# A quarter of the weight groups: the low part from a negated copy and two accumulating DMAs

## The chip, the cores and the metric

The kernel runs on one core of a Trainium2 chip. A core has five engines that run their own instruction queues side by side: TensorE (PE in the profile, its weight loads PEld), VectorE (DVE), ScalarE (ACT), GpSimd (POOL) and SyncE (SP, which here only issues DMAs). Sixteen DMA engines move data between HBM and the on-chip memory SBUF. Products accumulate in PSUM. DMAs can be issued from the queues of SP, ACT and POOL; an instruction at the head of a queue that waits holds up all that stands behind it.

The metric is the time of one execution in device microseconds (us). Two runs of the kernel before gave 1782.39 and 1782.95 us, median 1782.67.

## What is computed

One decoder layer for 256 tokens of width 2048, all in float32: a SwiGLU feed-forward network (FFN) of hidden width 5632, a mixer (pooling and gated linear attention behind one joint projection), and a second FFN. Cut to its frame:

```python
def swiglu(h, w_in, w_out):
    gu = h @ w_in                                   # 2048 x 11264
    gate, up = gu[..., :D_FF], gu[..., D_FF:]
    return (jax.nn.silu(gate) * up) @ w_out         # 5632 x 2048

h = h + 0.5 * swiglu(rmsnorm(h, ffn1_norm[l]), ffn1_w_in[l], ffn1_w_out[l])
u = rmsnorm(h, mix_norm[l]) @ w_in_mix[l]           # 2048 x 4112
...
h = h + jnp.concatenate([y_pool, y_gla], axis=-1) @ w_out_mix[l]
h = h + 0.5 * swiglu(rmsnorm(h, ffn2_norm[l]), ffn2_w_in[l], ffn2_w_out[l])
return rmsnorm(h, final_norm)
```

Nearly all of the work is products of 256 tokens with large weight matrices, and each weight is read from HBM once.

## The kernel before

**Split products.** TensorE takes float32 operands as two `float32r` parts: `hi` is the value rounded to 12 significant bits, `lo` the rest, so that `hi + lo` is the value. Each product is accumulated in PSUM as `a_hi*hi + a_hi*lo + a_lo*hi`, where `a` stands for the activations and `hi`, `lo` for the weights. The activations are the stationary operand (128 features by 128 tokens), the weights stream past them, 512 columns at a time.

**Groups.** A weight group is two adjacent K tiles (`KG = 2`, 256 rows) of 512 columns, 512 KB. `weights()` (from line 69) fetches one: line 73 issues one DMA from SP's queue into `raw`, line 86 makes `hi` with a rounding copy on ScalarE (a CAST in the profile), line 87 makes `lo = raw - hi` with a subtraction on VectorE. `raw`, `hi` and `lo` (`wr_`, `wh_`, `wl_` in the profile) come from a pool with `bufs=4`: each has four buffers in turn, and the fifth group's copy has to wait until the first group's buffer is free. `hi` and `lo` come free when TensorE has finished the group, `raw` when the copy and the subtraction have read it.

**Products.** `project()` (line 98) goes over the groups of one 512-column chunk. For each it calls `weights()` and then issues, for both token tiles and both K tiles, the three matmuls of line 110: 12 matmuls a group, in the order hi, lo, hi for the first K tile, then the second, for the first token tile, then the same for the second token tile. A product over K = 2048 has 8 groups, one over K = 5632 has 22.

**Stages.** First FFN: for each of 11 column chunks a `gate` and an `up` product (`f1g`, `f1u`), then four chunks of the way out (`ps_h`, 22 groups each; `residual()`, line 250). Mixer: products `mgr` (336 columns), `mk`, `mq`, `mv`, `mg` (352 columns), `mp` of 8 groups each, the last three twice, with small work between them, then its way out (four chunks of 8 groups, again `ps_h`). Second FFN: `f2g`, `f2u` and `ps_h` as in the first. The very first product has its first group cut in two. In all that makes 633 groups. In the last chunk of the last product the final six groups are held in buffers of another pool (`hold`), so that the token tiles can be finished one after the other.

**GpSimd** has little to do: a power in each row factor (line 154), small input DMAs (lines 310 to 321 and 512 to 514), the key product `ktail` (line 385), the final gains' DMAs and scaling (lines 573 and 580), and six multiplications with them (line 268).

The order of the instructions on each engine is set by the tile framework's scheduler from the program order and its own estimate of the times; semaphores guard every tile that is shared between engines or with a DMA.

Of the kernel before, what the change touches and what calls it, by code (L numbers as in the profile page):

```python
"""Macaron decoder layer (SwiGLU, pooling + gated-linear-attention mixer, SwiGLU) on one core.

Every large product takes float32 operands as two float32r parts that add up to them exactly
(hi = the value rounded to 12 significant bits, lo = the rest) and accumulates
hi*hi + hi*lo + lo*hi in PSUM. Activations are stationary (features on the partitions, tokens in
the columns), weights stream past them 512 columns at a time. The RMSNorm's per-token factor
commutes with the product and is applied where its result leaves PSUM; the gain is applied where
the activations are transposed.
"""
# [8 lines left out]
F32 = mybir.dt.float32  # L18
# [4 lines left out]
ALU = mybir.AluOpType  # L23
PSUM = bass.MemoryType.PSUM

P = 128
T = 256
# [23 lines left out]
def layer(ctx: ExitStack, tc: tile.TileContext, io):  # L51
# [13 lines left out]

# [1 line left out]
    last_load = [None]  # L67

    def weights(w, rows, c0, cw, name, hold):
        """The K tiles `rows` (adjacent) of w's columns c0..c0+cw as (hi, lo)."""  # L70
        n = len(rows)
        raw = wpool.tile([P, KG, CW], F32, tag="wraw", name=f"wr_{name}")
        dma = nc.sync.dma_start(
            out=raw[:, :n, :cw],
            in_=w[rows[0] * P : (rows[0] + n) * P, c0 : c0 + cw].rearrange(
                "(k p) c -> p k c", p=P
            ),
        )
        last_load[0] = dma.ins
        if hold:  # L80
            hi = block([P, KG, CW], F32R, f"wh_{name}")
            lo = block([P, KG, CW], F32R, f"wl_{name}")
        else:
            hi = wpool.tile([P, KG, CW], F32R, tag="whi", name=f"wh_{name}")
            lo = wpool.tile([P, KG, CW], F32R, tag="wlo", name=f"wl_{name}")
        nc.scalar.copy(out=hi[:, :n, :cw], in_=raw[:, :n, :cw])  # L86
        nc.vector.tensor_tensor(  # L87
            out=lo[:, :n, :cw],
            in0=raw[:, :n, :cw],
            in1=hi[:, :n, :cw].bitcast(F32),  # L90
            op=ALU.subtract,
        )
        return hi, lo
# [4 lines left out]
    def project(act, groups, w, c0, cw, name, apart=0, midway=None):  # L98
        """act.T @ w[:, c0:c0+cw] for both token tiles, in PSUM; act(kt) gives (hi, lo) [P, T].
        Over the last `apart` groups the first token tile is finished ahead of the second, and  # L100
        the second's left half ahead of its right; midway() is called behind the fourth group."""
        ps = [ps_acc.tile([P, CW], F32, tag="acc", name=f"ps_{name}_{t}") for t in range(NT)]
# [28 lines left out]

# [1 line left out]
    h = [hpool.tile([P, D], F32, tag=f"h{t}", name=f"h{t}") for t in range(NT)]  # L133
# [6 lines left out]
    def scaled_split(hi, lo, src, col):  # L140
        """hi + lo = src * col (per partition); hi, lo float32r, src [P, n]."""
        nc.scalar.activation(out=hi, in_=src, func=AF.Copy, scale=col)  # L142
        nc.vector.scalar_tensor_tensor(
            out=lo, in0=src, scalar=col, in1=hi.bitcast(F32), op0=ALU.mult, op1=ALU.subtract
        )

    def rms_factor(ss, n, cols, name):
        """(ss / n + EPS) ** -0.5 for [P, cols]; one Newton step on top of the power."""
        v = small.tile([P, cols], F32, tag=f"rv{cols}", name=f"{name}_v")
# [19 lines left out]
    def row_factor(ss, name):  # L169
        """ss [P, NT, 4]: sums of squares by token tile and column chunk."""  # L170
        tot = small.tile([P, NT], F32, tag="tot", name=f"{name}_tot")
        nc.vector.tensor_reduce(out=tot, in_=ss, axis=mybir.AxisListType.X, op=ALU.add)
        return rms_factor(tot, D, NT, name)

    # Products of nothing bring TensorE's clock up while the first loads are on their way.
    zeros = tmp.tile([P, CW], BF16, tag="sil", name="zeros")
# [4 lines left out]

# [1 line left out]
    neg_half = const.tile([P, 8], F32, name="neg_half")  # L183
# [12 lines left out]
    def transposed_rows(src, hi, lo, cols, name):  # L196
        """hi, lo [P, 4, T] from src[t] [P, 512] (token-major), times cols [P, 4]."""
        for k2 in range(2):
            tp = ps_t.tile([P, 2, T], F32, tag="tp", name=f"tp_{name}_{k2}")
            for k in range(2):  # L200
                for t in range(NT):
                    kk = k2 * 2 + k
                    nc.tensor.transpose(  # L203
                        tp[:, k, t * P : (t + 1) * P], src[t][:, kk * P : (kk + 1) * P], ident
                    )
            for k in range(2):
                kk = k2 * 2 + k
                scaled_split(hi[:, kk, :], lo[:, kk, :], tp[:, k, :], cols[kk])

    def ffn_in(w, act, row, name, first=None):  # L210
        """The gated hidden activations; row() gives the row factors once the second product is
        under way."""
        g_hi, g_lo = [], []
# [36 lines left out]
    def residual(act, order, w, factor, gain, name, extra=None):  # L250
        """h += factor * act.T @ w; the new h's transposed parts and row factors."""
        hi, lo = new_hT(name) if gain is not None else (None, None)
# [23 lines left out]

    # ================= first FFN =================
    # x arrives transposed, group by group with the first weights, and behind them as it is.
    first = [[0], [1]] + [[k, k + 1] for k in range(2, KD, 2)]
# [33 lines left out]

    # ================= mixer =================
    w_in = io["w_in_mix"]
# [9 lines left out]

    # decay: gate_lr and the tail of the output gate
    gsil = [block([P, HEADS * DV], F32, f"gsil{t}") for t in range(NT)]
# [17 lines left out]
    for t in range(NT):  # L345
# [3 lines left out]
        z.append(zt)  # L349
    # log_sigmoid(z) = min(z, 0) - ln(1 + exp(-|z|))  # L350
    nc.scalar.activation(out=e, in_=e, func=AF.Exp, scale=-1.0)
# [5 lines left out]

    # exp of the cumulated log decays: transposed (E1, and E2 for its inverse), and of what is
    # left of the chunk behind a token (token-major). tri holds 1/16 where it isn't zero.
    E1 = block([P, HEADS, T], F32, "E1")  # L360
# [17 lines left out]

    # keys
    ps = project(hact, kd, w_in, O_K, CW, "mk")  # L380
# [22 lines left out]

    # queries
    ps = project(hact, kd, w_in, O_Q, CW, "mq")
# [8 lines left out]

    # scores, transposed (keys on the partitions), masked to j <= i within a chunk
    sT = block([P, NT, HEADS, P], F32, "sT")
# [9 lines left out]

    # values
    v = [block([P, HEADS * DV], F32, f"v{t}") for t in range(NT)]
# [6 lines left out]

    # states in front of chunks 1..3
    st = [block([P, HEADS, DV], F32, f"st{n}") for n in range(1, 4)]
# [21 lines left out]

    # the rest of the output gate  # L460
    for c in range(2):
# [6 lines left out]

    # attention outputs, normalized and gated
    y_hi, y_lo = [None] * 4, [None] * 4  # L470
    y = [block([P, HEADS * DV], F32, f"y{t}") for t in range(NT)]
    for t in range(NT):
        so = small.tile([P, HEADS], F32, tag="so", name=f"so{t}")
        po = []
        for hp in range(2):
            o = ps_t.tile([P, 2, DV], F32, tag="tp", name=f"o{t}_{hp}")
            for j in range(2):
# [3 lines left out]
                for cc in range(2):  # L481
                    n = 2 * t + cc
                    if n == 0:
                        continue  # nothing precedes chunk 0
                    nc.tensor.matmul(
# [20 lines left out]

    # pooling: the windows' means minus the token are a product with a banded matrix
    band = [block([P, 2, 3 * P], F32, f"band{i}") for i in range(2)]
# [14 lines left out]
    for i in range(2):  # L523
# [8 lines left out]
        for j in range(2):  # L532
            pp = ps_t.tile([P, 2, T], F32, tag="tp", name=f"pp{i}_{j}")
            for c in range(2):
# [3 lines left out]
                )  # L538
                # Windows reach REACH tokens into the second tile: the columns before it are
                # overwritten, those of the reach added to.  # L540
                nc.tensor.matmul(
# [26 lines left out]

    # ================= second FFN and the final norm =================
    g = ffn_in(io["ffn2_w_in"], hact, lambda: rstd, "f2")  # L570
# [6 lines left out]

    # gf holds the gains over -2, as the Newton step gives -2 times the row factor.
    for n in range(4):
        nc.gpsimd.tensor_scalar_mul(gf[n], gf[n], -0.5)  # L580

    def finish(ps, ss):
        """The last column chunk, by halves; the row factors and the result."""
        half = CW // 2
# [52 lines left out]
def _constants(np):  # L637
    """Matrices that depend on shapes alone: cumulation within a chunk (with the decay's 1/16), and
    trailing-window means minus the token, both with the summed token on the partitions."""
    s, t = np.arange(P)[:, None], np.arange(P)[None, :]  # L640
# [53 lines left out]
```

## Time and profile before

| what | value |
|---|---|
| time, median of 2 runs | 1782.67 us |
| span of the profiled execution, first to last instruction | 1780.9 us |
| mean granted TensorE clock | 0.999 of full speed |
| VectorE's subtractions in `weights()` | 633, 768 us in all |
| ScalarE's rounding copies in `weights()` | 633, 659 us in all |
| GpSimd busy | 35.1 us |
| DMA engines busy (mean of 16), rate | 60%, 190 GB/s |
| moved by DMA | 338 MB, of it 3.06 MB from GpSimd's queue |

The profile is one execution recorded on the chip; the time of that execution itself was not given apart from its span, which is 1.8 us under the median of the timed runs. In a row such as "L86 ACT CAST wh_h<-wr_h ... x208 | 218.9, 1054 | 301.4 <-PE ps_h L110 274.5" stand the line of the kernel, the engine and its operation, output and input tile, the count, the busy time in us, the mean of one in ns, and behind the second bar the time the engine was idle before these instructions with what ended most of it. In the table of waits a row is "who waits <- for whom: us in total, times, longest". In the tables of a tile or line, a row gives the count, the least, median and greatest duration in ns and the start of the first and the last in us. "DMA to landing" counts from the issue of a DMA until its data is there. A stretch of time is given as from:to, its length, the busy time of each engine with the number of its instructions, the granted TensorE clock, the share of the DMA engines' time and the rate in GB/s. TensorE's matmuls overlap: one is shown with 389 ns, but a new one starts every 227 ns.

### The profile page before, as it was taken

How to read it: one execution, taken by the hardware profiler on the slowest of the kernel's cores; microseconds unless marked ns; L12 is line 12 of the kernel's file. 1: busy time of each engine (PE TensorE's matmuls, PEld its weight loads, DVE VectorE, ACT ScalarE, POOL GpSimd, SP SyncE). 2: the span in 40 equal slices, each digit the busy share in tenths (PEclk: the TensorE clock that was granted, in tenths of full speed). 3: DMA queues.
4: the chain of work that ended last, by engine and by line, in shares of the span. 5: the costliest groups of instructions: out<-in, count | busy, mean ns of one | idle time of the engine just before them, and what ended most of it. 6: DMA issues, size and time to landing. Idle time of an engine off the chain costs nothing.

```text
span 1780.9 us, 20687 instructions
## 1 busy us (share of the span) xinstructions
PE 1768.4 (99%) x8086; PEld 1467.1 (82%) x8086; DVE 894.8 (50%) x902; ACT 791.2 (44%) x911; POOL 35.1 (2%) x40
## 2 busy tenths in 40 slices
PE   9999999999999999999999999999999999999998
PEld 6888888888888888878978888888888888888886
DVE  5544444444555445544455554444444555554454
ACT  6444444444444444454445544444444444443443
POOL 0000000000000000000010000000000000200000
PEclk9999999999999999999999999999999999999999
DMA  9666666666565655555554566666666666766653
GB/s 310 202 189 189 189 190 189 189 189 189 190 190 190 197 190 189 175 171 171 173 193 145 188 188 189 189 190 189 189 189 189 189 189 190 215 194 193 192 196 133
DMA packets 176449, 338.01 MB, mean 190 GB/s; under 512 B 10807, under 2 KB 19255, under 8 KB 176096
## 3 DMA queue, kind: packets, MB, share of 16 engines
q1 hardware_dynamic: 174976, 333.10, 59.5%
q0 software_dynamic: 944, 3.06, 0.6%
q8 instruction: 63, 1.03, 0.2%
q10 hardware_dynamic: 432, 0.55, 0.1%
q14 instruction: 34, 0.28, 0.0%
HBM read 334.56 MB, written 2.10 MB: 189 GB/s over the span
## 4 chain that ended last, share of the span: by engine, by line
PE 98%; issue 0%; DMA 0%; DVE 0%; ACT 0%; SPq 0%; POOLq 0%; POOL 0%; DVEq 0%
PE ps_h L110 31%; PE ps_f2g L110 13%; PE ps_f2u L110 13%; PE ps_f1u L110 13%; PE ps_f1g L110 13%; PE ps_mp L110 3%; PE ps_mv L110 2%; PE ps_mg L110 2%; PE ps_mk L110 1%; PE ps_mq L110 1%; PE ps_mgr L110 1%; PE f2tp L240 1%; PE f1tp L240 1%; PE tp_h L203 0%; DMA wr_f1g<-in_ffn_w_in 0%
## 5 line engine op out<-in xcount | busy, mean ns | idle before, releaser
L87 DVE TENSOR_TENSOR wl_h<-wr_h,wh_h 128x1024 fp32r<-128x1024 f32 x208 | 256.8, 1236 | 269.9 <-ACT wh_h L86 269.7
L86 ACT CAST wh_h<-wr_h 128x1024 fp32r<-128x1024 f32 x208 | 218.9, 1054 | 301.4 <-PE ps_h L110 274.5
L87 DVE TENSOR_TENSOR wl_f2u<-wr_f2u,wh_f2u 128x1024 fp32r<-128x1024 f32 x88 | 107.8, 1225 | 131.5 <-ACT wh_f2u L86 131.5
L87 DVE TENSOR_TENSOR wl_f1u<-wr_f1u,wh_f1u 128x1024 fp32r<-128x1024 f32 x88 | 107.8, 1225 | 129.2 <-ACT wh_f1u L86 129.1
L87 DVE TENSOR_TENSOR wl_f2g<-wr_f2g,wh_f2g 128x1024 fp32r<-128x1024 f32 x88 | 107.8, 1225 | 102.1 <-ACT wh_f2g L86 102.1
L87 DVE TENSOR_TENSOR wl_f1g<-wr_f1g,wh_f1g 128x1024 fp32r<-128x1024 f32 (+1 forms) x89 | 108.0, 1213 | 98.9 <-ACT wh_f1g L86 98.5
L86 ACT CAST wh_f2g<-wr_f2g 128x1024 fp32r<-128x1024 f32 x88 | 92.8, 1055 | 126.8 <-PE ps_f2u L110 66.6
L86 ACT CAST wh_f2u<-wr_f2u 128x1024 fp32r<-128x1024 f32 x88 | 92.7, 1053 | 122.6 <-PE ps_f2u L110 66.9
L86 ACT CAST wh_f1g<-wr_f1g 128x1024 fp32r<-128x1024 f32 (+1 forms) x89 | 93.0, 1045 | 119.1 <-PE ps_f1u L110 63.2
L86 ACT CAST wh_f1u<-wr_f1u 128x1024 fp32r<-128x1024 f32 x88 | 92.6, 1052 | 116.1 <-PE ps_f1u L110 61.9
L110 PE MATMUL ps_f1g<-wh_f1g,xT_hi 128*128 128x512 f32 x352 | 137.1, 394 | 2.5 <-ACT xT_hi L142 2.4
L110 PE MATMUL ps_h<-wh_h,f2hi 128*128 128x512 f32 (+1 forms) x364 | 139.2, 382 | 0.0
L110 PE MATMUL ps_h<-wh_h,f2lo 128*128 128x512 f32 (+1 forms) x364 | 139.1, 382 | 0.0
L110 PE MATMUL ps_h<-wl_h,f2hi 128*128 128x512 f32 (+1 forms) x364 | 139.1, 382 | 0.0
L110 PE MATMUL ps_f2g<-wh_f2g,h_hi 128*128 128x512 f32 x352 | 138.0, 392 | 0.0
L110 PE MATMUL ps_h<-wh_h,f1hi 128*128 128x512 f32 x352 | 137.3, 390 | 0.0
L110 PE MATMUL ps_h<-wl_h,f1hi 128*128 128x512 f32 x352 | 137.2, 390 | 0.0
L110 PE MATMUL ps_f2g<-wh_f2g,h_lo 128*128 128x512 f32 x352 | 137.1, 389 | 0.0
L110 PE MATMUL ps_f2g<-wl_f2g,h_hi 128*128 128x512 f32 x352 | 137.1, 389 | 0.0
L110 PE MATMUL ps_h<-wh_h,f1lo 128*128 128x512 f32 x352 | 137.0, 389 | 0.0
L110 PE MATMUL ps_f1u<-wl_f1u,xT_hi 128*128 128x512 f32 x352 | 136.9, 389 | 0.0
L110 PE MATMUL ps_f1u<-wh_f1u,xT_lo 128*128 128x512 f32 x352 | 136.9, 389 | 0.0
(225 smaller groups left out, 3323.8 us busy)
## 6 DMA issues: line engine op xcount, KB each, us to landing
wr_h<-in_ffn_w_out SPq DMA_DIRECT2D x176, 512.0 KB, 3.9
wr_f1u<-in_ffn_w_in SPq DMA_DIRECT2D x88, 512.0 KB, 3.5
wr_f2g<-in_ffn_w_in SPq DMA_DIRECT2D x88, 512.0 KB, 3.4
wr_f2u<-in_ffn_w_in SPq DMA_DIRECT2D x88, 512.0 KB, 3.4
wr_f1g<-in_ffn_w_in SPq DMA_DIRECT2D x87, 512.0 KB, 3.5
wr_h<-in_w_out_mix SPq DMA_DIRECT2D x32, 512.0 KB, 4.0
wr_mv<-in_w_in_mix SPq DMA_DIRECT2D x16, 512.0 KB, 3.6
wr_mp<-in_w_in_mix SPq DMA_DIRECT2D x16, 512.0 KB, 4.5
```

Source lines behind the costliest of these rows:

```text
L86: nc.scalar.copy(out=hi[:, :n, :cw], in_=raw[:, :n, :cw])
L87: nc.vector.tensor_tensor(out=lo[:, :n, :cw], in0=raw[:, :n, :cw], in1=hi[:, :n, :cw].bitcast(F32), op=ALU.subtract,)
L110: nc.tensor.matmul(ps[t][:, c], a[:, s], b[:, j, c], start=kt == first and i == 0, stop=kt == last and i == 2, skip_group_check=c.start > 0,)
L240: nc.tensor.transpose(tp[:, k, :], a[:, k * P : (k + 1) * P], ident)
```

## The change

Every fourth call of `weights()` that isn't held no longer subtracts on VectorE. Instead ScalarE writes `-hi` into `lo` behind the rounding copy, and two DMAs from GpSimd's queue, one for each K tile, read the weights from HBM a second time and add them to `lo` (`accum_op=ALU.add`), which leaves `w - hi` there. The other three quarters of the groups are treated as before. The diff, without the comments and docstrings that it also drops:

```diff
     last_load = [None]
+    count = [0]
 
     def weights(w, rows, c0, cw, name, hold):
         n = len(rows)
         raw = wpool.tile([P, KG, CW], F32, tag="wraw", name=f"wr_{name}")
...
         nc.scalar.copy(out=hi[:, :n, :cw], in_=raw[:, :n, :cw])
+        count[0] += 1
+        if count[0] % 4 == 0 and not hold:
+
+            nc.scalar.mul(lo[:, :n, :cw], hi[:, :n, :cw].bitcast(F32), -1.0)
+            for j in range(n):
+                nc.gpsimd.dma_start(
+                    out=lo[:, j, :cw],
+                    in_=w[(rows[0] + j) * P : (rows[0] + j + 1) * P, c0 : c0 + cw],
+                    accum_op=ALU.add,
+                )
+            return hi, lo
         nc.vector.tensor_tensor(
             out=lo[:, :n, :cw],
             in0=raw[:, :n, :cw],
```

## The prediction, made before the changed kernel ran

> **What bounds the kernel now.** I read the page from the top (busy times, slices, the chain that ended last), then the table of waits.
>
> ```profile
> span 1780.9 us, 20687 instructions
> PE 1768.4 (99%) x8086; PEld 1467.1 (82%) x8086; DVE 894.8 (50%) x902; ACT 791.2 (44%) x911; POOL 35.1 (2%) x40
> PEclk9999999999999999999999999999999999999999
> PE 98%; issue 0%; DMA 0%; DVE 0%; ACT 0%; SPq 0%; POOLq 0%; POOL 0%; DVEq 0%
> ...
> PE ps_f1g L110 <- ACT xT_hi L142: 2.4, 2, 1.4
> ...
> ACT wh_h L86 <- PE ps_h L110: 274.5, 174, 3.0
> ```
>
> TensorE (PE) is busy for 99% of the span at full granted clock and makes up 98% of the chain. All its waits for the first x tiles come to 2.4 us; ScalarE (ACT) waits for TensorE, not the other way round. So relieving VectorE (DVE) gives nothing back: all that is left to win are the 1780.9 - 1768.4 = 12.5 us in which TensorE is idle. The question is only whether `lo` now comes too late.
>
> The beat stands in ScalarE's timeline; a group's spare time in the rows of the second FFN's `up` weights between 1100 and 1500 us:
>
> ```profile
> 1600.38 1.05 ACT L86 CAST wh_h<-wr_h 128x1024 fp32r<-128x1024 f32 x1 [1.67 <-PE ps_h L110]
> 1603.10 1.05 ACT L86 CAST wh_h<-wr_h 128x1024 fp32r<-128x1024 f32 x1 [1.67 <-PE ps_h L110]
> ...
> L86 ACT CAST wh_f2u<-wr_f2u x72: 1041/1055/1055, 1101.7 to 1476.2; 128x1024 fp32r<-128x1024 f32 x72
> L87 DVE TENSOR_TENSOR wl_f2u<-wr_f2u,wh_f2u x72: 1224/1225/1227, 1102.8 to 1477.2; 128x1024 fp32r<-128x1024 f32 x72
> ...
> L110 PE MATMUL ps_f2u<-wl_f2u,h_hi x288: 389/389/389, 1109.9 to 1486.4; 128*128 128x512 f32 x144
> ```
>
> A cast starts every 2.72 us, released by TensorE: a group of 12 matmuls takes 2.72 us, 0.227 us for one. With `bufs=4` a cast starts when the group four before it is finished, so three groups, 8.2 us, lie between the cast and its own group's matmuls. The rows agree: the first cast starts at 1101.7, the first matmul that takes its `lo` at 1109.9. Today `lo` is ready at 1102.8 + 1.2 = 1104.0, 5.9 us early. **Deadlines from the start of the cast:** 8.2 us for `lo[:, 0]` (second matmul of a group), and three matmuls (0.7 us) more, 8.9 us, for `lo[:, 1]` (fifth matmul).
>
> **How many groups change.** The subtraction (line 87) runs once a group; over the whole span its busy time and its count (and below it a row that ScalarE's part needs):
>
> ```profile
> 0.00:1781.00 1781.00, 768.29 (x633) 1.00 0.60 190
> ...
> L351 ACT ACTIVATE e<-e x1: 1061/1061/1061, 769.2 to 769.2; 128x1024 f32<-128x1024 f32 x1
> ```
>
> 633 groups; every fourth is 158, of which numbers 628 and 632 are among the last six, which are held and stay as they are: **156 groups**. As `bufs` is 4 too, it is always the same `lo` buffer. A changed group that comes late holds TensorE; the next changed one can start its cast only when that group is done, again 8.2 us ahead of its need. So lateness isn't made up for in between, nor does it grow: the cost is 156 times the lateness of one group.
>
> **VectorE: removed.** 156 subtractions of 1.2 us, 190 us. Worth nothing, as the subtraction is 5.9 us early and TensorE the bound. The wait of the next load's issue (SP) for that subtraction goes too; the cast releases the raw buffer 1.2 us sooner, also hidden.
>
> **ScalarE: added.** 156 negated copies of 128x1024. The nearest row is the 128x1024 ACTIVATE of line 351, 1.06 us: 165 us, which fit into the 1.67 us of each 2.72 in which ScalarE waits for TensorE. Only the next group's cast stands behind a copy, and it waits until 2.72 us anyway. As latency it counts: cast 1.06, copy 1.06, a hand-over of about 0.1: the first transfer can be issued 2.2 us after the cast began.
>
> **The two accumulating transfers: added.** The trace holds none. The nearest rows are plain transfers from GpSimd's (POOL's) queue: their median landings by size, the spread of landings of the `gf` and `wp` ones (the line below each), and two stretches with DMA share and GB/s at the end of the line:
>
> ```profile
> wp<-in_w_pool POOLq DMA_DIRECT2D x4, 256.0 KB, 6.9
> gf<-in_final_norm POOLq DMA_DIRECT2D x4, 256.0 KB, 4.9
> band<-in_band POOLq DMA_DIRECT2D x2, 384.0 KB, 5.1
> pscale<-in_pscale POOLq DMA_DIRECT2D x1, 4.0 KB, 3.6
> ...
> L573 POOL DMA_DIRECT2D gf<-in_final_norm x4: 583/587/610, 1515.4 to 1535.1; - x4
> DMA to landing us min/median/max: 3.9/4.9/5.3
> ...
> L512 POOL DMA_DIRECT2D band<-in_band x2: 552/592/631, 918.4 to 920.4; - x2
> L514 POOL DMA_DIRECT2D wp<-in_w_pool x4: 709/720/738, 919.0 to 921.7; - x4
> DMA to landing us min/median/max: 3.7/6.9/8.6
> ...
> 926.00:928.00 2.00, 2.00 (x16) 1.83 (x15) 1.50 (x2) 1.94 (x5) 0.00 (x0) 1.00 1.02 375
> 1100.00:1500.00 400.00, 400.00 (x1803) 331.93 (x1802) 200.01 (x181) 172.96 (x181) 0.00 (x0) 1.00 0.61 190
> ```
>
> By the 4 KB row a landing is about 3.6 us that don't depend on size, plus bytes over the rate that the weight loads leave: 375 GB/s with all engines busy, less 190, is 185. For 256 KB (0.262 MB) that gives 3.6 + 1.4 = 5.0 us; the lone `gf` row has 4.9. The burst of `band` and `wp` (1.83 MB) got more: if the longest landing is the last one's, it lasted from 918.4 to 921.7 + 8.6 = 930.3, and less the 3.6 that is 1.83 MB in 8.3 us, 220 GB/s.
>
> *Lower bound, priced as two plain copies at 185 GB/s:* the first lands at 2.2 + 5.0 = 7.2 us, 1.0 before its deadline; the second (issued 0.6 us later, behind the first's bytes) at 2.2 + 3.6 + 0.524/0.185 = 8.6 us, 0.3 before its own. Hidden, just. Nothing below that can win time, as TensorE is busy anyway.
>
> *Upper bound:* each takes twice the longest landing of the burst, one behind the other, 2.2 + 2 x 8.6 = 19.4 us, 10.5 late: 156 x 10.5 = 1640 us more.
>
> *What I take:* an add has to read what it adds to. So beside 0.262 MB from HBM each transfer also reads 0.262 MB of `lo`: its reads are those of two copies. The first then lands at 2.2 + 3.6 + 0.524/0.220 = 8.2 us, on its deadline (8.6 us at 185 GB/s); the second at 2.2 + 3.6 + 1.049/0.220 = 10.6 us, **1.7 us late**. At 185 GB/s it would be 11.5, but while TensorE waits the loads wait too and leave more; four loads of 0.524 MB spread over 10.9 + 1.9 us leave 211 GB/s, which makes it 1.9 late. I keep 1.7, nearer to the copies than to the upper bound, since the burst's row is the only one with several such transfers in flight.
>
> So plain copies would be hidden and a doubled read would not. The Trainium skill speaks against the change here (Collectives: The Full Stack, "The bandwidth ceiling: the fold count and why AG ≠ RS ≠ AR"): of an add made by the DMA engines it says that the add is free but its two source reads on one ring halve the rate, 62.28 against 32.35 GB/s. By that factor of 1.93 the second transfer would be some 1.5 us late, an estimate from that page; no run here shows an accumulating transfer yet.
>
> **The sum over the groups.** 150 groups of full width x 1.7 = 255 us. Six (in `mgr` and `mg`) are narrower:
>
> ```profile
> 748.04 0.75 ACT L86 CAST wh_mgr<-wr_mgr 128x672 fp32r<-128x672 f32 x1 [1.13 <-PE ps_mgr L110]
> 749.88 1.05 ACT L86 CAST wh_mk<-wr_mk 128x1024 fp32r<-128x1024 f32 x1 [1.09 <-PE ps_mgr L110]
> ```
>
> Their period is 1.84 us, so the time ahead shrinks by 3 x 0.88 = 2.6 us and the second deadline by 0.2 more, while cast and copy save 0.6 and the fewer bytes 1.6: 1.7 + 2.6 + 0.2 - 0.6 - 1.6 = 2.3 late, 6 x 2.3 = 14 us.
>
> **GpSimd's queue.** 312 issues at 0.6 to 0.7 us (the rows above), 200 us on an engine that is 2% busy. But issues are in order, so an accumulating pair can stand behind this work:
>
> ```profile
> L268 POOL TENSOR_TENSOR h<-h,gf 128x512 f32<-128x512 f32 x6 | 8.7, 1478 | 165.9 <-ACT sq_h L167 113.9 <-issue 52.1
> L580 POOL TENSOR_SCALAR gf<-gf 128x512 f32<-128x512 f32 x4 | 7.2, 1791 | 17.1 <-DMA gf<-in_final_norm 17.1
> L385 POOL TENSOR_TENSOR ktail<-k_sb,Es 128x512 f32<-128x512 f32 x2 | 2.6, 1308 | 40.4 <-ACT k_sb L384 40.3
> ```
>
> 8.7 + 7.2 + 17.1 (the scaling waits for its rows at the head of the queue) + 2.6 = 36 us if every such moment met a pair; pairs come every 11 us, so I take 10, with 0 and 36 as ends. The other way round, the power in a row factor may wait behind a pair that waits for its copy, some us: the four accumulators in PSUM let TensorE go on with the next product meanwhile.
>
> **The loads and the DMA engines.** 81 MB more from HBM and as many reads of `lo`. Of the engines' time 61% is taken; 1.05 MB more per 10.9 us is 96 GB/s, about a quarter of 375: 0.87. The loads share the engines:
>
> ```profile
> wr_h<-in_ffn_w_out SPq DMA_DIRECT2D x176, 512.0 KB, 3.9
> ...
> wr_mp<-in_w_in_mix SPq DMA_DIRECT2D x3, 512.0 KB, 6.5
> ```
>
> (the second in the 20 us around the burst). A load is issued behind the subtraction, 2.3 us after its group's cast began, and is needed by the cast four groups on, 10.9 us after it: 8.6 us for 3.9 to 6.5. They stay hidden, by 2.1 us at the least.
>
> Sum: 1782.7 + 255 + 14 + 10 = **2062 us**. The profiled span is 1780.9, so 1.8 us lie outside it; the sum stands on the median of the runs, 1782.67.
>
> **Rivals.** *Hidden after all:* the engines read `lo` beside the stream at no price, and the transfers land like copies. For it: the lower bound misses no deadline, and the 256 KB rows land in 3.9 at best. Against: the second has 0.3 us to spare, less than the spread from 3.9 to 5.3. It decides at a landing of the second 8.9 us after the cast. Then only the queue's collisions are left: 1783 to 1815, not slower. The Trainium skill (DMA: Bandwidth & Descriptors, "Anatomy of one DMA — SWDGE (gpsimd) path") has 2.0 us plus bytes at 436 GB/s, which also leads here; the trace's 4.9 us for 256 KB disagrees.
>
> *Accumulating much slower than two copies:* read, add and write one after the other, three passes. The second then lands at 2.2 + 3.6 + 1.57/0.220 = 12.9 us, 4.0 late: 1782.7 + 156 x 4.0 = 2410; by the upper bound 3420. And then the clock may fall:
>
> ```profile
> 1771.89 0.28 PE L110 MATMUL ps_h<-wh_h,f2lo 128*128 128x256 f32 x1
> ...
> 1774.00:1776.00 2.00, 0.00 (x0) 0.00 (x0) 1.35 (x5) 0.72 (x1) 0.55 (x1) 1.00 0.00 0
> 1776.00:1778.00 2.00, 0.00 (x0) 0.00 (x0) 0.58 (x1) 0.00 (x0) 0.00 (x0) 0.76 0.84 314
> ```
>
> TensorE's last matmul ends at 1772.2; its granted clock (0.76, next to the last two columns) is still whole until 1776 and falls in the next 2 us. Waits under 4 us should leave it alone, longer ones would add up to 2.7 us to the group behind. For it: nothing in the trace bounds an add. Against: nothing either.
>
> *Faster:* none of TensorE's work goes, so over 35 us can't be won.
>
> **How the numbers follow.** Forecast (0.6 to 3.5 us late, 1890 to 2340): 0.54, 2062 the likeliest. Hidden: 0.19. Much slower: 0.26. Faster: 0.01. Runs of this kernel tell about 2% (36 us, 0.23 us a group) from no change. The range for 8 in 10 takes in hidden, forecast and the near end of much slower: 1782 to 2450. Faster 0.01, within 2% 0.19, slower 0.80.
>
> **What would show it.** A new wait of PE's `ps_` rows for the transfers into `wl_`, some 150 times, 1.7 us each; two landings per group of about 6 and 8 us from issue, not 5 and 6; ScalarE's copies x156 at 1.06; 477 subtractions; GpSimd's queue from 3 MB to 84 or 165; the clock at 1.00. Landings under 6 us, or TensorE still at 98%, make it wrong on the one side, landings over 11 us on the other.

## The result and the profile after

The changed kernel takes **1852.87 us** (median of 2 runs, 1848.44 and 1857.3) against 1782.67 us: 1.039 times as long, with a 95% interval of 1.0335 to 1.0453. It is slower, as forecast, but by 70 us and not by 279.

First the head of the page of the changed kernel (busy times, clock, DMA queues, shares of the chain that ended last). In it the rounding copy is line 87, the negated copy line 91, the accumulating transfers line 93, the subtraction line 99 and the matmul line 122.

```profile
span 1855.5 us, 21444 instructions
PE 1798.1 (97%) x8086; PEld 1461.6 (79%) x8086; DVE 714.3 (38%) x746; ACT 950.8 (51%) x1067; POOL 306.4 (17%) x352
PEclk8999999999999999999999999999999999999999
q1 hardware_dynamic: 174976, 333.10, 55.6%
q0 software_dynamic: 45872, 83.85, 28.3%
PE 65%; DMA 24%; ACT 6%; issue 2%; POOL 2%; DVE 0%; SPq 0%; ACTq 0%; POOLq 0%; DVEq 0%
```

TensorE executes the same 8086 matmuls, but DMA now makes up 24% of the chain, where it had 0%. The work moved as the diff says: VectorE has 156 instructions fewer (902 to 746), ScalarE 156 more (911 to 1067), GpSimd 312 more (40 to 352). Next TensorE's table of waits, the rows for transfers into `lo` that come first (total us, times, longest):

```profile
PE ps_h L122 <- DMA wl_h<-in_ffn_w_out: 12.8, 22, 2.1
PE ps_f1g L122 <- DMA wl_f1g<-in_ffn_w_in: 9.6, 6, 7.0
PE ps_f2u L122 <- DMA wl_f2u<-in_ffn_w_in: 7.7, 9, 1.6
PE ps_f1u L122 <- DMA wl_f1u<-in_ffn_w_in: 5.2, 8, 1.6
```

These are the new waits that the prediction asked for, but 45 of them in these rows and not some 150, and most shorter than 1.7 us. The table is short of the loss, because a matmul is shown with 389 ns and the next may start after 227: of each wait the first 0.16 us look like work. Counted from start to start, what TensorE lost in gaps over 0.3 us grew from 15.2 to 87.0 us; these 72 us are nearly all of the 74.6 us between the two profiled spans (the one of the changed kernel, 1855.5, is an execution somewhat longer than the median). They take in the matmuls that ran at half the clock, which start 0.44 us apart (below). The second row hides the worst one: 7.0 of `ps_f1g`'s 9.6 us are a single wait.

The changed groups of the second FFN's `up` product between 1100 and 1500 us (count, then min/median/max in ns), and under them the landings of their transfers:

```profile
L93 POOL DMA_DIRECT2D wl_f2u<-in_ffn_w_in x36: 862/865/1222, 1113.7 to 1490.0; - x36
L91 ACT ACTIVATE wl_f2u<-wh_f2u x18: 1061/1062/1063, 1112.3 to 1488.1; 128x1024 fp32r<-128x1024 f32 x18
...
DMA to landing us min/median/max: 4.2/6.0/9.1
```

The negated copy has the forecast 1.06 us. The landings mix first and second transfers. Told apart over all 156 changed groups, from the trace's records (medians in us):

```
                         first: issue to landing / from cast    second: issue to landing / from cast
changed kernel           5.29 / 7.77                            6.58 / 9.57
forecast                 6   / 8.2                              8    / 10.6
negated copy's end 2.15 after the cast's start; from there to the first issue 0.29; to the second issue 0.54 more
```

**One group in the timeline** (start, duration, and in brackets the idle time before it and what ended it):

```profile
1431.15 1.05 ACT L87 CAST wh_f2u<-wr_f2u 128x1024 fp32r<-128x1024 f32 x1 [1.71 <-PE ps_f2g L122]
...
1432.23 1.06 ACT L91 ACTIVATE wl_f2u<-wh_f2u 128x1024 fp32r<-128x1024 f32 x1
...
1433.59 1.75 POOL L93 DMA_DIRECT2D wl_f2u<-in_ffn_w_in  x2 [9.13 <-PE ps_f2g L122]
...
1439.90 0.47 PE L122 MATMUL ps_f2u<-wl_f2u,h_hi 128*128 128x512 f32 x1 [0.22 <-DMA wl_f2u<-in_ffn_w_in]
```

From cast to first issue 2.44 us; a matmul that takes `lo` waits 8.75 us after the cast, and only 0.22 us visibly. ScalarE still waits 1.71 us for TensorE ahead of the cast, so the copy costs it nothing. Such a group is nearly on time; the next part shows the one that isn't.

**The first changed group.** It is the fourth group of the kernel, in the fill:

```profile
11.81 1.05 ACT L87 CAST wh_f1g<-wr_f1g 128x1024 fp32r<-128x1024 f32 x1 [0.28 <-DMA wr_f1g<-in_ffn_w_in]
...
13.58 1.04 ACT L91 ACTIVATE wl_f1g<-wh_f1g 128x1024 fp32r<-128x1024 f32 x1
...
14.92 1.86 POOL L93 DMA_DIRECT2D wl_f1g<-in_ffn_w_in  x2 [10.91 <-ACT wl_f1g L91]
...
22.08 0.77 PE L122 MATMUL ps_f1g<-wl_f1g,xT_hi 128*128 128x512 f32 x1 [7.02 <-DMA wl_f1g<-in_ffn_w_in]
```

The cast is released by its load and not by TensorE: the work has no lead yet, and the transfer's whole time stands on the path. The stretches around it (length, busy us and instructions of PE, PEld, DVE, ACT, POOL, then the granted clock, DMA share and GB/s):

```profile
14.00:18.00 4.00, 1.06 (x5) 0.55 (x3) 2.60 (x5) 4.00 (x7) 1.86 (x2) 0.98 1.09 361
18.00:22.00 4.00, 0.00 (x0) 0.00 (x0) 4.00 (x10) 3.55 (x8) 0.00 (x0) 0.50 1.10 295
22.00:26.00 4.00, 3.92 (x9) 3.17 (x10) 1.08 (x1) 0.00 (x0) 0.00 (x0) 0.50 1.05 349
26.00:30.00 4.00, 4.00 (x15) 3.23 (x14) 0.00 (x0) 2.10 (x2) 0.81 (x2) 0.74 0.35 89
```

The granted clock falls to 0.50 in the wait, stays there for the next 4 us of work (9 matmuls in 3.92 us) and is 0.74 in the 4 us behind them. The kernel before has whole clock and 19 or 20 matmuls in each of these four stretches.

### The profile page after: what moved, and what is told of

The parts are those of the page before. It is cut to its first block, busy times and chain, and to the rows that moved or that the text cites. A ratio compares the mean times of both kernels' runs of the same rounds, so it can differ in the third digit from the quotient of the medians.

```text
span 1855.5 us, 21444 instructions
## 1 busy us (share of the span) xinstructions
PE 1798.1 (97%) x8086; PEld 1461.6 (79%) x8086; DVE 714.3 (38%) x746; ACT 950.8 (51%) x1067; POOL 306.4 (17%) x352
## 3 DMA queue, kind: packets, MB, share of 16 engines
q0 software_dynamic: 45872, 83.85, 28.3%
## 4 chain that ended last, share of the span: by engine, by line
PE 65%; DMA 24%; ACT 6%; issue 2%; POOL 2%; DVE 0%; SPq 0%; ACTq 0%; POOLq 0%; DVEq 0%
PE ps_h L122 18%; PE ps_f2g L122 11%; PE ps_f1u L122 9%; PE ps_f1g L122 9%; DMA wl_h<-in_ffn_w_out 9%; PE ps_f2u L122 9%; DMA wl_f1g<-in_ffn_w_in 3%; DMA wl_f2u<-in_ffn_w_in 3%; PE ps_mv L122 2%; DMA wl_f2g<-in_ffn_w_in 2%; DMA wl_f1u<-in_ffn_w_in 2%; PE ps_mg L122 1%; ACT wh_h L87 1%; ACT wl_h L91 1%; PE ps_mp L122 1%
## 5 line engine op out<-in xcount | busy, mean ns | idle before, releaser
L99 DVE TENSOR_TENSOR wl_h<-wr_h,wh_h 128x1024 fp32r<-128x1024 f32 x158 | 196.2, 1243 | 328.2 <-ACT wh_h L87 328.1
L122 PE MATMUL ps_f1g<-wl_f1g,xT_hi 128*128 128x512 f32 x352 | 140.0, 399 | 10.1 <-DMA wl_f1g<-in_ffn_w_in 9.6
L122 PE MATMUL ps_f2u<-wl_f2u,h_hi 128*128 128x512 f32 x352 | 138.2, 393 | 7.8 <-DMA wl_f2u<-in_ffn_w_in 7.7
L99 DVE TENSOR_TENSOR wl_f1u<-wr_f1u,wh_f1u 128x1024 fp32r<-128x1024 f32 x66 | 80.9, 1225 | 164.8 <-ACT wh_f1u L87 164.8
L99 DVE TENSOR_TENSOR wl_f2u<-wr_f2u,wh_f2u 128x1024 fp32r<-128x1024 f32 x66 | 80.9, 1226 | 163.6 <-ACT wh_f2u L87 163.6
L122 PE MATMUL ps_f1g<-wh_f1g,xT_lo 128*128 128x512 f32 x352 | 138.6, 395 | 0.0
L122 PE MATMUL ps_f2u<-wh_f2u,h_lo 128*128 128x512 f32 x352 | 137.1, 390 | 0.0
```

The lines of the kernel that those rows point to most:

```text
L99: nc.vector.tensor_tensor(out=lo[:, :n, :cw], in0=raw[:, :n, :cw], in1=hi[:, :n, :cw].bitcast(F32), op=ALU.subtract,)
L122: nc.tensor.matmul(ps[t][:, c], a[:, s], b[:, j, c], start=kt == first and i == 0, stop=kt == last and i == 2, skip_group_check=c.start > 0,)
```

## The experiments

The theory after the result: the transfers land later than copies would because of the add, but some 1 us earlier than forecast, and TensorE needs the second K tile's `lo` later than forecast. The second part comes from the order of the products, which the scheduler made anew. Where the first use of the first and of the second K tile's `lo` stands among the 12 matmuls of a group, counted in the kernels' instruction lists:

```
before              all groups                2nd and 5th
changed kernel      113 of 156 changed groups 3rd and 9th
                     34                       2nd and 5th
                      9                       elsewhere
e.g. of f2u: hi.t0 hi.t1 lo0.t0 hi.t0 hi.t0 lo0.t1 hi.t1 hi.t1 lo1.t0 ...   (t: token tile; lo0, lo1: K tile of lo)
```

In 113 groups the second `lo` is thus needed 8.2 + 7 x 0.227 = 9.8 us after the cast, not 8.9. Rivals: the landings alone explain the smaller loss; or most of the loss lies in the fill.

### Copies in place of adds

```diff
-                    accum_op=ALU.add,
```

> The two transfers of a changed group copy the weights over lo and add nothing (lo is then the whole weight, so the output is another one); order, bytes from HBM and issues are those of the changed kernel. If the add doubles the transfers' reads, as the forecast had it, their share of the engines halves (28.3% to about 14%) and the second lands some 1.5 us sooner, about 8.2 us after the cast instead of 9.6: next to no group is late, 1785 to 1800 us. Rival: the landings are latency of GpSimd's queue and of its descriptors, and reading lo costs little: second landing still over 9 us, 1835 us or more.

Measured: 1796.82 us (1795.51 to 1797.85), 1.0082 [1.0064, 1.0100], in the range; the queue's share fell to 16.4% and not to 14%. The copies land 4.34 and 4.46 us after issue (medians), 6.78 and 7.44 after the cast. The second `lo` stands 9th as often as in the changed kernel, so the order of the products is not what differs. Its page (busy times, queue), its first wait on a transfer, and rows of its line 93:

```profile
PE 1772.2 (99%) x8086; PEld 1466.8 (82%) x8086; DVE 713.1 (40%) x746; ACT 951.0 (53%) x1067; POOL 198.1 (11%) x352
...
q0 software_dynamic: 45872, 83.85, 16.4%
```

```profile
PE ps_f1g L121 <- DMA wl_f1g<-in_ffn_w_in: 6.2, 1, 6.2
```

```profile
L93 POOL DMA_DIRECT2D wl_h<-in_ffn_w_out x84: 527/535/593, 505.9 to 1752.2; - x84
...
DMA to landing us min/median/max: 2.9/4.4/7.1
```

So the add is what makes the transfers late: 56 of the 70 us go with it. Of the 14 left, one wait of 6.2 us is the first changed group again; by the first transposes' start (65.7 us, before 57.0) the fill costs 8.7 us. The add's price on the DMA engines: the same 83.85 MB took 16.4% of 1793.7 us, 294 us of all engines, as copies, and 28.3% of 1855.5 us, 525 us, as adds: **1.79 times**. That fits a second read; no run here separates it from another way in which an add could keep the engines longer.

### The negated copy alone

Lines 92 to 97, the loop with both transfers, are taken out.

> The changed groups keep ScalarE's negated copy and lose both transfers (lo stays -hi, so the add is left out). If the transfers make the whole cost: 1780 to 1786 us, TensorE waiting for nothing. Rival: the copies on ScalarE, or the altered order of the work, carry part of it: 1795 us or more.

Measured: 1786.49 us (1784.92 to 1788.8), 1.0021 [1.0012, 1.0031], 0.5 us above the theory's range. 156 copies on ScalarE, without their subtractions, cost some 4 us (2 to 5.5 by the interval). TensorE's waits:

```profile
PE ps_f1g L116 <- ACT xT_hi L148: 2.3, 2, 1.4
PE ps_h L116 <- ACT up L533: 2.0, 1, 2.0
```

The first is that of before (2.4 us), the second a new one in the mixer, of 2.0.

### A fifth buffer for hi and lo

```diff
-    tmp = ctx.enter_context(tc.tile_pool(name="tmp", bufs=3))
+    tmp = ctx.enter_context(tc.tile_pool(name="tmp", bufs=2))
...
-            hi = wpool.tile([P, KG, CW], F32R, tag="whi", name=f"wh_{name}")
-            lo = wpool.tile([P, KG, CW], F32R, tag="wlo", name=f"wl_{name}")
+            hi = wpool.tile([P, KG, CW], F32R, tag="whi", name=f"wh_{name}", bufs=5)
+            lo = wpool.tile([P, KG, CW], F32R, tag="wlo", name=f"wl_{name}", bufs=5)
```

> hi and lo get five buffers instead of four (and two small temporaries two instead of three, to make room), so a changed group has 2.7 us more ahead of its need. If the cost is lateness against that need: landings stay near 9.6 us after the cast, the need moves to 11 us and beyond, only the first groups still wait: 1785 to 1800 us. Rival: the second read of the weights takes the DMA engines away from the loads, or slows them as a whole: no gain, 1840 us or more.

Measured: 1802.90 us (1802.04 to 1809.82), 1.0122 [1.0101, 1.0144]: 3 us above the range. Page (queue) and waits:

```profile
q0 software_dynamic: 45872, 83.85, 28.9%
```

```profile
PE ps_f1g L122 <- DMA wl_f1g<-in_ffn_w_in: 8.3, 2, 7.2
PE ps_h L122 <- DMA wl_h<-in_ffn_w_out: 3.9, 3, 2.6
```

The transfers cost the engines what they did, and the second lands 9.57 us after the cast as before; what the edit moves is the need (`tmp` has a buffer fewer beside it), and 50 us went with it. For a group's first matmul it moves by nearly a group's 2.72 us, from 7.9 to 10.7 us after the cast (medians of the trace). For the second `lo` it moves by 1.8, from 9.8 to 11.6, because the scheduler, with five buffers, left the second `lo` 5th in all but some ten of the changed groups. So it is their lateness against TensorE, and not the traffic, that costs. The wait in the fill stays (7.2 us).

### The products in the written order

Each matmul of line 122 is tied behind the one before it in the program:

```diff
+    behind = [None]
...
+                    if behind[0] is None:
+                        behind[0] = product().ins
+                    else:
+                        with tc.issue_after(behind[0]):
+                            behind[0] = product().ins
```

(`product()` returns the matmul of before.)

> TensorE's products are held in the order in which the kernel writes them; the scheduler had put the second K tile's lo from the fifth to the ninth matmul in 113 of the 156 changed groups. If that order is why the groups were less late than forecast: the need of the second lo falls back to 8.9 us after the cast, the landings stay, and summing what the changed kernel's landings exceed 8.2 and 8.9 us by gives 132 us: 1905 to 1930 us. Rival: the order doesn't matter and the forecast failed by the landings alone: 1845 to 1860 us.

Measured: 1919.74 us (1913.01 to 1929.33), 1.0773 [1.0728, 1.0819], in the range. Now `lo` is first used in all groups 2nd and 5th, as the prediction had it, and the loss is 137 us. Page and waits:

```profile
PE 1819.6 (95%) x8086; PEld 1464.8 (77%) x8086; DVE 714.8 (37%) x746; ACT 951.3 (50%) x1067; POOL 307.0 (16%) x352
```

```profile
PE ps_h L124 <- DMA wl_h<-in_ffn_w_out: 34.8, 43, 1.8
PE ps_f1g L124 <- DMA wl_f1g<-in_ffn_w_in: 11.4, 12, 5.5
```

The way out waits 43 times and 34.8 us, not 22 times and 12.8. The second transfer lands 9.46 us after the cast, so it isn't later; it is needed earlier.

### Written order, with copies

The two edits above together.

> The transfers copy and add nothing (lo is then the whole weight), and TensorE's products are held in the written order. If holding the order costs only where a transfer is late: copies land 7.5 us after the cast, the need is 8.9, so as with the copies in the scheduler's order, 1793 to 1800 us. Rival: the held order costs by itself, and part of what it added to the adding transfers was its own: 1810 us or more.

Measured: 1802.93 us (1801.81 to 1804.35), 1.0114 [1.0099, 1.0129], between the two ranges. Against the copies alone it is 6 us longer, so about 6 of the 67 us between the changed kernel and the held order are the holding's own, if it costs the same with late transfers, and some 60 are the need that comes 0.9 us earlier.

### 4 KB transfers: what doesn't depend on size

```diff
+                extra = dict(accum_op=ALU.add) if j == 1 else {}
...
-                    out=lo[:, j, :cw],
-                    in_=w[(rows[0] + j) * P : (rows[0] + j + 1) * P, c0 : c0 + cw],
-                    accum_op=ALU.add,
+                    out=lo[:, j, :8],
+                    in_=w[(rows[0] + j) * P : (rows[0] + j + 1) * P, c0 : c0 + 8],
+                    **extra,
```

> Each of the two transfers carries 8 columns instead of 512 (4 KB), the first a copy, the second an add; the rest of lo stays -hi. It shows the part of a landing that doesn't depend on size, in the middle of the run. If the forecast's 3.6 us hold, both land 3.6 us or more after issue, and its mistake was the rate. Rival: the 3.6 us were the crowd of the first microseconds; then both land in 2.0 to 2.9 us, the add not far behind the copy. Time 1783 to 1792 us either way.

Measured: 1791.69 us (1.0050 [1.0034, 1.0066]). The copy lands 3.28 us after its issue, the add 2.94 (medians). Rows of the transfers' line (the least and the greatest duration are those of copy and add), and the first wait:

```profile
L94 POOL DMA_DIRECT2D wl_h<-in_ffn_w_out x84: 545/731/947, 505.1 to 1748.3; - x84
...
DMA to landing us min/median/max: 1.9/3.2/6.3
```

```profile
PE ps_f1g L123 <- DMA wl_f1g<-in_ffn_w_in: 5.7, 1, 5.7
```

The fixed part is 2.9 to 3.3 us, between the 3.6 of the forecast and the rival's 2.0 to 2.9, and an add, here always the second of the pair, has none of its own beyond a copy's. Of the 9 us lost, 5.7 stand in this wait; by the first transposes' start (64.5 us) the fill costs 7.5. After it, 156 copies and 312 issues on GpSimd cost some 2 us as long as the data comes early.

### The change from the 20th group on

```diff
-        if count[0] % 4 == 0 and not hold:
+        if count[0] % 4 == 0 and count[0] > 16 and not hold:
```

> The first 16 groups are split as before the change, so 152 groups change instead of 156. If the 15 us that the changed kernel had lost by its first transposes are a cost of the first fill of the pipeline, where the loads come together and the first changed group has no lead: 12 to 15 us less than the changed kernel, 1836 to 1842 us. Rival: they are four ordinary late groups: 2 to 4 us less.

Measured: 1830.25 us (1825.41 to 1832.36), 1.0270 [1.0253, 1.0287]. Four changed groups fewer save 22 us, more than I expected. By the first transposes' start (57.7 us, 71.9 in the changed kernel) 14 of them lie in the fill, as expected; where the other 8 come from is not settled, since the executions of the changed kernel alone spread over 15 us. The first 30 us of the kernel before, the changed kernel and this one, in this order:

```profile
0.00:30.00 30.00, 26.22 (x102) 18.81 (x103) 19.35 (x30) 18.92 (x29) 3.04 (x10) 1.00 0.89 290
```

```profile
0.00:30.00 30.00, 18.35 (x57) 12.00 (x58) 13.20 (x25) 17.13 (x27) 5.70 (x14) 0.83 0.88 275
```

```profile
0.00:30.00 30.00, 26.25 (x95) 18.71 (x96) 19.35 (x30) 18.98 (x29) 3.05 (x10) 0.94 0.90 300
```

57 matmuls against 102 and 95: the fill comes back. The clock of 0.94 here, without a changed group in the stretch, stays unexplained; with the negated copies alone, and no transfer at all, it is 0.57 from 12 to 16 us, as in this kernel.

### Every eighth group

```diff
-        if count[0] % 4 == 0 and not hold:
+        if count[0] % 8 == 0 and not hold:
```

> Every eighth group changes (78). If each changed group pays its own lateness and nothing carries over: half of the 55 us outside the start, and a start that costs less, since the first changed group is the eighth: 1812 to 1822 us. Rival: the DMA engines as a whole are what is short, so that lateness is carried from one changed group to the next; then half the load removes nearly all of it: under 1800 us.

Measured: 1804.91 us (1802.78 to 1809.2), 1.0127 [1.0112, 1.0142], between theory and rival. By the first transposes' start 3.4 of the 22 us are lost in the fill; the other 19 over 78 groups are 0.24 us each, against (70 - 22)/152 = 0.31 for every fourth group (0.36 with the 15 us that the same measure gives for the fill there). So the cost goes by the number of changed groups only roughly: each costs a quarter to a third less. The second transfer lands 9.24 us after the cast, not 9.42 and 9.57 as in the two profiled executions with every fourth group; that is the likely reason, but it was not tried apart.

### The changed kernel again

No edit; it ran beside the two above.

> The changed kernel itself, on this chip beside the others: 1848 to 1858 us.

Measured: 1852.70 us (1840.7 to 1855.65), 1.0379 [1.0343, 1.0415]. In its profiled execution, the 1840.7, the landings exceed the forecast's deadlines of 8.2 and 8.9 us by 109 us in all; in the one shown above it is 132. One execution's sum is no better than that.

### Fifth buffer and later start together

> Five buffers for hi and lo and the first 16 groups as before, together. If lateness against the need and the first fill are the whole cost, next to nothing is left: 1783 to 1793 us. Rival: what five buffers left (20 us) is the price of the transfers' traffic: 1798 us or more.

Measured: 1795.15 us (1792.9 to 1796.15), 1.0066 [1.0049, 1.0083], above the theory's range and below the rival's. TensorE's first waits:

```profile
PE ps_h L122 <- ACT up L539: 2.8, 1, 2.8
PE ps_h L122 <- DMA wl_h<-in_ffn_w_out: 2.5, 3, 1.2
...
PE ps_f1g L122 <- DMA wl_f1g<-in_ffn_w_in: 1.8, 1, 1.8
...
PE ps_mg L122 <- DMA wl_mg<-in_w_in_mix: 1.1, 2, 0.6
```

Both causes taken away leave 12.7 us: 5.4 in these waits for transfers, 2.8 for ScalarE in the mixer, and behind the latter the granted clock is 0.55 from 951.0 to 954.8 us, some 1.7 us more. What makes up the rest I have not settled.

### One transfer for both K tiles

```diff
-            for j in range(n):
-                nc.gpsimd.dma_start(
-                    out=lo[:, j, :cw],
-                    in_=w[(rows[0] + j) * P : (rows[0] + j + 1) * P, c0 : c0 + cw],
-                    accum_op=ALU.add,
-                )
+            nc.gpsimd.dma_start(
+                out=lo[:, :n, :cw],
+                in_=w[rows[0] * P : (rows[0] + n) * P, c0 : c0 + cw].rearrange(
+                    "(k p) c -> p k c", p=P
+                ),
+                accum_op=ALU.add,
+            )
```

> One accumulating transfer of both K tiles instead of two of one. The same bytes, one issue and one landing less. If it is the landing against the need that costs: now the first lo too has to wait for all the bytes, which land some 9.4 us after the cast, against a need at 8.4: about 1.1 us for each of 156 groups and the start, 1940 to 2000 us. Rival: bytes and issues set the time: as the changed kernel or better, 1835 to 1855 us.

Measured: 1976.82 us (1966.18 to 1991.13), 1.1094 [1.1039, 1.1149], in the range. Rows of its transfers (line 92), and its first wait:

```profile
L92 POOL DMA_DIRECT2D wl_h<-in_ffn_w_out x42: 1194/1203/1281, 554.6 to 1920.3; - x42
...
DMA to landing us min/median/max: 4.7/6.7/9.4
```

```profile
PE ps_h L123 <- DMA wl_h<-in_ffn_w_out: 46.2, 31, 2.6
```

The same bytes with half the issues are much slower. The one transfer lands 6.7 us after its issue, 9.2 after the cast; some 120 of the 156 groups use it 3rd, 8.4 us after the cast, and even the first K tile has to wait for all bytes. When each part is needed decides, and not the bytes or the issues. In the trace this lateness sums to 155 us. The rest of the 194 us holds the fill, 17 by the first transposes' start, and the clock: behind waits of 1.8 to 3.2 us it falls to 0.50 eleven times after the fill, for 3.4 us each time. One of them:

```profile
436.00:439.00 3.00, 0.90 (x4) 0.46 (x3) 1.23 (x1) 1.02 (x1) 0.00 (x0) 1.00 0.85 262
439.00:442.00 3.00, 3.00 (x8) 2.36 (x8) 0.00 (x0) 0.00 (x0) 0.00 (x0) 0.51 0.64 196
```

## Why the prediction was wrong

**What held.** TensorE is the bound, and VectorE's relief is worth nothing: with the 156 subtractions gone and nothing added but the copies the kernel isn't faster. ScalarE's copies, 1.06 us each, are hidden but for some 4 us. Copies in place of the adds would nearly have been hidden: forecast 7.2 and 8.6 us after the cast, measured 6.78 and 7.44. An add costs the engines nearly what two copies do: forecast as the reads of two copies, measured 1.79 times the engines' time of a copy. The factor of 1.93 that the Trainium skill gives (Collectives: The Full Stack, "The bandwidth ceiling: the fold count and why AG ≠ RS ≠ AR") is near it. That the reason is a second read is not shown apart. No wait on a weight load is among TensorE's first ones. Neither rival came: the transfers miss their deadline, and an add isn't three passes.

**First failing step: the landing** ("the second at 2.2 + 3.6 + 1.049/0.220 = 10.6 us, 1.7 us late"). It came 9.57 us after the cast. By its terms: the issue is 2.44 us after the cast, not 2.2 (0.24 later). The fixed part is about 3.1 us, between the 2.9 and 3.3 of the 4 KB transfers, and not the 3.6 of one row at the kernel's start (0.5 earlier). What is left, 9.57 - 2.44 - 3.1 = 4.03 us for 1.049 MB, is 260 GB/s; the burst of `band` and `wp` gave 220 (0.74 earlier); both rates count the read of `lo` as bytes, as the forecast did. So the term 1.7 was really 0.7 at the median. The forecast's own rows spoke against its 3.6 and 220: they give 4.8 us for 256 KB, and the least landing of `wp` was 3.7. By its own signs (landings of about 6 and 8 us, not 5 and 6) the measured 5.29 and 6.58 lie on the side of the copies. A linear sum at the edge of a deadline is so sensitive: a tenth off the landing takes more than half of the lateness. The landings measured in all 156 groups, held against the forecast's own deadlines of 8.2 and 8.9 us, sum to 132 us of lateness; the kernel with the written order, where these deadlines hold, measured 137. That the two agree so closely is luck: this kernel's own landings, in its trace, sum to 111, and its 137 us also hold a fill of 17 (by the first transposes' start), the holding's own 6 and stretches of low clock. The forecast had 255 + 14 + 10. From 2062 to 1919.7 us this step is 142 us, net of these costs that the forecast left out.

**Second failing step: the deadline** ("three matmuls (0.7 us) more, 8.9 us, for `lo[:, 1]` (fifth matmul)"). That was read from the order of before, and the scheduler wrote another one: 9.8 us in 113 groups. From 1919.7 to 1852.8 us this is 67 us, about 6 of them the holding's own. The same landings, against each group's own positions, sum to 58 us without the first four groups, and 43 in the other profiled execution; measured without these groups are 48. That the scheduler moved the products because it takes the transfers for late is likely: copies in place of the adds get the same order, and with a fifth buffer the old one mostly comes back. Why 113 groups and not all was not tried.

**Third, the other way: the fill** ("again 8.2 us ahead of its need", so "the cost is 156 times the lateness of one group"). The first changed groups have no lead; TensorE waits 7.0 us for the first, and the clock falls to 0.50 behind it. With the first four left out, 22 of the 70 us are gone, 14 of them in the fill. The prediction had "the clock at 1.00", which holds nearly everywhere else (mean 0.995), and named a rule for the rival alone, that waits under 4 us should leave the clock alone. The rule is wrong here: behind a wait of 2.1 us for `wl_h`, which ends at 656.2 us, the clock falls as well, and the changed kernel does 4 and 7 matmuls in 2 us instead of 8 or 9.

```profile
654.00:656.00 2.00, 0.02 (x1) 0.00 (x0) 1.79 (x3) 0.91 (x3) 0.00 (x0) 1.00 0.97 290
656.00:658.00 2.00, 1.85 (x4) 1.49 (x5) 0.22 (x1) 0.00 (x0) 0.00 (x0) 0.53 0.84 271
658.00:660.00 2.00, 2.00 (x7) 1.60 (x6) 0.00 (x0) 0.16 (x1) 0.00 (x0) 0.62 0.28 93
```

**GpSimd's queue** (10 us, 0 to 36) was not measured by itself. With copies and with the 4 KB transfers, which issue as often, some 5 and 2 us are left after the fill, so it is at the low end where the data comes early.

The bound, the sign and the kind of loss (transfers that miss TensorE's need) were right. The forecast was 209 us too high because the lateness of one group came out as 1.7 us and was 0.31 in the mean, on two separate counts, landing and deadline; the fill, which it had at nothing, hid 14 to 22 us of that error.

## What to carry to other kernels

When the cost is a small difference of two large times, landing less deadline, carry the uncertainty of both through the sum: here 1 us of landing was worth some 140 us, and 0.9 us of deadline some 60. Read the deadline from the order of the instructions in the changed kernel; a scheduler may write another order around a slower operand, and a fifth buffer won 50 of 70 us with landings unchanged. Check the first passes of a loop apart from the steady state: there a transfer's full time stands on the path, and an idle TensorE is slow for some time after.

## What the runs showed of the hardware

An accumulating DMA into SBUF from GpSimd's queue, 256 KB beside steady loads, lands 5.3 us (first) and 6.6 us (second, issued 0.54 us later) after its issue, a copy 4.3 and 4.5. The record of its issue is longer, but that does not hold GpSimd longer: rows of line 93 of the changed kernel, to be held against the 535 ns of the copies above:

```profile
L93 POOL DMA_DIRECT2D wl_h<-in_ffn_w_out x84: 853/891/1255, 520.8 to 1813.7; - x84
...
DMA to landing us min/median/max: 3.5/6.0/9.1
```

The second issue of a pair starts 0.54 us after the first with adds and 0.52 with copies (medians), so records of adds overlap; in the timeline above two of them take 1.75 us together. The longer record doesn't come from the bytes: the 4 KB adds took about as long (up to 947 ns in the row above). And the queue's 83.85 MB count an add's bytes once; what more it costs shows only in the engines' time.

The granted clock fell to about 0.50 behind waits much shorter than the 7.0 us in the fill: in the changed kernel once more, for 3.4 us behind the wait of 2.1 us, and eleven times with one transfer for both K tiles. It did not fall behind each such wait: the kernel with the later start kept its whole clock behind one of 3.0 us at 1554 us.
